# A two-layer hybrid transformer step on one core: where a finished pair of attention heads is split into its two product parts

## The chip, the cores and the metric

The kernel runs on one core of a Trainium2 chip, one launch per run. The metric is the device time of a run in microseconds (us). Before the change the median of three runs is 1104.95 us (1104.42 to 1105.27). The core has five engines that work through their own queues in order: TensorE (PE in the profile, with the loading of its weights shown apart as PEld), VectorE (DVE), ScalarE (ACT), GpSimd (POOL) and SyncE (SP), which here issues nearly all transfers.

## What is computed

Two layers on 512 tokens of width 1024 in float32. Both mix tokens, project with `w_out`, add, and run a gated feed-forward. The parts that the change touches are the two attentions (shapes and names are shortened):

```python
def memory_attention(q_mem, mem_n, w_mem_kv):          # 4 heads of 64, in both layers
    k, v = split(mem_n @ w_mem_kv)                     # 256 memory rows
    p = softmax(einsum('bshd,bmhd->bhsm', q, k) * 64 ** -0.5)
    return einsum('bhsm,bmhd->bshd', p, v)

def forgetting_attention(q, k, v, log_f):              # 12 heads of 64, layer 2 only
    c = cumsum(log_f)
    logits = einsum('bthd,bshd->bhts', q, k) * 64 ** -0.5 + c_t - c_s
    p = softmax(where(s <= t, logits, -inf))           # causal
    return einsum('bhts,bshd->bthd', p, v)

mixed = concatenate([main, memory_attention(...)], axis=-1)
h = h + rmsnorm(mixed @ w_out[layer], ln_mix_post[layer])
```

In layer 1 `main` is a gated spatial mix, in layer 2 it is the forgetting attention.

## The kernel before

**Products in parts.** A float32 product is taken as three products of a high and a low part (`mm3`, L189 to L193). So everything that enters a product is first *split* (`split`, L238): ACT copies the tile to the rounded high part, then DVE subtracts it to get the low part. Splits of weights are `whi`/`wlo` from `raw`, of turned probabilities `pT` from `tr`, of finished heads `mixedhi`/`mixedlo` from `f`. `last_parts` holds the two instructions of the last split written.

**Two heads per tile.** A head's output fills 64 of 128 rows. `join` (L414) adds the two halves of the output bank `o` (or `mo`) into one tile `f` that two heads, a pair, share. After the second head of a pair it hands back a function, the split of the finished `f` into `mixedhi` and `mixedlo`. There are two pairs in layer 1 and eight in layer 2 (two of the memory heads, six of the forgetting heads).

**The schedule of heads.** `attend` (L538) walks through the heads by a list of steps, and in one round it does the first half of head `u` and the second half of the head before it, `r`:

- `S3 S2 S1 S0` are the logits of `u` (PE, bank `lg`, two products each of 512, 384, 256 and 128 columns) with the row maximum (DVE, L443) and the exponential (ACT, L445); `N3 N2 N1 N0` scale the probabilities `p` by the reciprocal of their sum (DVE, L452 and L457, one of them on ACT, L455).
- `T0 T1 T2` turn the probabilities of `r` (PE transposes into `tr`, L464) and split the turned block into `pT`; `V0 V1 V2` are its products with the values (PE, L532, into `o`). `V2` ends with `join`.
- `F0` to `F4` are places for other work: pieces of the key, value and output projections (PE, with the splits of their weights), and the making of the next head's operands (`head_parts`, L1347: six copies of 128 KB and two of 4 KB into `qa`, `ka`, `qc`, `kc`, issued by SP).

Before the change the split of a finished pair is put into the list `late` and written at the next place for other work, which after `V2` is `F4`, the last step of the same round.

**The order in the queues.** What is written is then ordered by a scheduler: it merges the writing order into one queue per engine, by when it thinks that operands and buffers are ready. `tc.issue_after` (in `behind`, L247) adds an order edge on an engine and no wait: what is written in its block comes behind the named instruction in the same engine's queue. So a change of the writing order moves other instructions too. In the queues the heads of layer 2 are called f0 to f11 below; the round of head f*n* is the one in which its logits are written. Finished pairs are 0 to 5, and pair *n* is finished in the round of f(2*n*+2).

**Buffers.** `tr` banks 2, `mm` and `lg` banks 3 each; `raw` weights 4; `whi` and `wlo` 8 each. The output projection (`out_part`, L895, products `y`) is spread over the last rounds as pieces of three products per two-part step, and reads the memory pairs and pairs 0 and 1; the last four pairs are read after all heads (`mix_tail`, L920).

Of the kernel before, what the change touches and what calls it, by code (L numbers as in the profile page):

```python
# [16 lines left out]
T = 512  # L17
# [23 lines left out]
def hybrid(ctx: ExitStack, tc: tile.TileContext, i: dict, out: bass.AP):  # L41
# [11 lines left out]
    last_load, last_exp, last_parts = [None], [None], [None, None]  # L53
# [192 lines left out]
    @contextmanager  # L246
    def behind(some):  # L247

        with ExitStack() as s:
            for ins in some:  # L250
                s.enter_context(tc.issue_after(ins.ins))
            yield
# [285 lines left out]
    def attend(heads, before={}, between={}):  # L538


        steps = ("T0", "S3", "F0", "T1", "S2", "N3", "F1", "V0", "S1", "N2", "T2", "F2", "S0", "N1", "V1", "N0",
                 "F3", "V2", "F4")
        r, late = None, []
        for n, u in enumerate(list(heads) + [None]):
            more = list(between.get(n, ()))
            due = [len(more) * (x + 1) // 5 for x in range(5)]
            ahead = list(before.get(n, ()))
            done = 0
            for what in steps:
                x = int(what[1])  # L550
                if what[0] == "F":
                    for f in late + ahead[:1] + more[done : due[x]]:
                        f()
                    late, ahead = [], ahead[1:]
                    done = due[x]
                elif what[0] in "SN":
                    if u:
                        (u.logits if what[0] == "S" else u.norm)(x)
                elif r and x in r.blocks:
                    rest = (r.transpose if what[0] == "T" else r.values)(x)  # L560
                    if rest:
                        late.append(rest)
            assert not ahead
            r = u
        for f in late:
            f()
# [22 lines left out]
    def layer_a():  # L589
# [55 lines left out]
        with tc.tile_pool(name="sgu", bufs=1) as lp:  # L645
# [59 lines left out]
            mem_kv.append(mem_project(0, xs, wk))  # L705
            mixed = [None] * KT
            attend(mem_heads(0, q, mixed), between={n: take(fill, c) for n, c in enumerate((4, 4, 4, 4))})
            with tc.issue_after(last_exp[0].ins):
                for vt in (*vg.values(), us[0]):
# [492 lines left out]
    def layer_b(phase, fp):  # L1202
# [178 lines left out]
        for n, c in zip(range(12, 17), (2, 3, 3, 4, 4)):  # L1381
            between[n] = take(more, c)
        assert not fill and not more
        attend(heads, before, between)
        return mix_tail(1, mixed, ys)

# [113 lines left out]
```

## Time and profile before

| what | value |
|---|---|
| median of three runs | 1104.95 us (1104.42 to 1105.27) |
| the profiled execution: time, span | 1104.7 us, 1103.0 us |
| mean granted TensorE clock | 0.999 |
| busy: DVE, ACT, POOL | 888.0 us, 679.6 us, 23.9 us |
| heads of layer 1 (first logits to last join) | about 49 to 87 us |
| heads of layer 2: forgetting heads f0 to f11 | first logits at 613.2 us, last join at 722 us |
| splits of finished pairs, `mixedhi` and `mixedlo` | 10 each, median 620 and 686 ns |

The profile shows one execution on the chip. In the timeline a row is: start in us from the span's start, duration in us, engine, line, operation, tiles written and read, shape, count, and in brackets the idle time of the engine just ahead of the row and what ended it. Matmuls are pipelined: a product of 512 columns is shown with some 0.4 us but the next one starts 0.23 us later, so the time that PE loses is read from start to start. In the table of stages the columns are, for each engine, its busy time and the number of its instructions.

### The profile page before, as it was taken

The page shows a single profiled execution, that of the slowest core. Times are in us where ns is not written, and L with a number is a line of the kernel's source. Part 1 is how long each engine was busy: PE and PEld are TensorE (multiplying, and loading weights), DVE is VectorE, ACT ScalarE, POOL GpSimd, SP SyncE. Part 2 cuts the span into 40 slices and gives each one's busy share as a digit, 9 for nine tenths or more (in the row PEclk, how much of TensorE's full clock was granted, in tenths as well). Part 3 has the DMA queues.
Part 4 walks back from the last instruction along what each step waited for, and adds up shares of the span by engine and source line. Part 5 has one row for each costly group of instructions (what it writes and reads, how often), then busy time and mean ns, then how long its engine had stood idle before and what let it go on. Part 6 is the DMA issues. An engine that isn't in the chain of part 4 may idle for free.

```text
span 1103.0 us, 19497 instructions
## 1 busy us (share of the span) xinstructions
PE 1095.4 (99%) x7363; PEld 1001.7 (91%) x7363; DVE 888.0 (81%) x1750; ACT 679.6 (62%) x1428; POOL 23.9 (2%) x40
## 2 busy tenths in 40 slices
PE   9999999999999999999999999999999999999998
PEld 8998889999899899998988998889999899899996
DVE  7879759897698588797968789868997698588776
ACT  7776578664365254477747788868665266255454
POOL 0000000000000000001000000000000000000000
PEclk9999999999999999999999999999999999999999
DMA  7521331334135133245222654531235134233232
GB/s 271 160 79 58 115 115 39 116 115 138 54 115 145 54 109 115 77 153 175 71 82 61 154 136 119 148 115 40 78 97 153 58 115 132 61 113 117 77 97 77
DMA packets 64021, 118.65 MB, mean 108 GB/s; under 512 B 5236, under 2 KB 40072, under 8 KB 63928
## 3 DMA queue, kind: packets, MB, share of 16 engines
q1 hardware_dynamic: 63032, 116.57, 35.0%
q8 instruction: 58, 0.95, 0.4%
q0 software_dynamic: 192, 0.52, 0.2%
q10 hardware_dynamic: 704, 0.32, 0.1%
q14 instruction: 35, 0.29, 0.1%
HBM read 105.23 MB, written 2.10 MB: 97 GB/s over the span
## 4 chain that ended last, share of the span: by engine, by line
PE 93%; DVE 3%; ACT 2%; DMA 1%; issue 1%; SPq 0%; DVEq 0%; ACTq 0%
PE y L191 10%; PE y L192 10%; PE y L193 10%; PE a L191 5%; PE a L193 5%; PE a L192 5%; PE ps L191 4%; PE ps L193 4%; PE ps L192 4%; PE x L193 3%; PE x L191 3%; PE x L192 3%; PE e L191 3%; PE e L193 3%; PE e L192 3%; PE v L191 2%
## 5 line engine op out<-in xcount | busy, mean ns | idle before, releaser
L239 ACT CAST whi<-raw 128x512 fp32r<-128x512 f32 x460 | 277.6, 620 | 260.8 <-PE y L193 118.5
L239 DVE TENSOR_TENSOR wlo<-raw,whi 128x512 fp32r<-128x512 f32 x460 | 307.5, 689 | 116.2 <-ACT whi L239 114.0
L191 PE MATMUL y<-whi,fhi 128*128 128x512 f32 (+1 forms) x356 | 139.7, 393 | 0.0
L193 PE MATMUL y<-whi,flo 128*128 128x512 f32 (+1 forms) x356 | 139.4, 392 | 0.0
L192 PE MATMUL y<-wlo,fhi 128*128 128x512 f32 (+1 forms) x356 | 139.3, 391 | 0.0
L193 PE MATMUL x<-xshi,wlo 128*128 128x256 f32 x320 | 89.9, 281 | 0.0
L191 PE MATMUL x<-xshi,whi 128*128 128x256 f32 x320 | 89.8, 281 | 0.0
L191 PE MATMUL a<-xshi,whi 128*128 128x256 f32 x320 | 89.8, 281 | 0.0
L192 PE MATMUL x<-xslo,whi 128*128 128x256 f32 x320 | 89.8, 281 | 0.0
L192 PE MATMUL a<-xslo,whi 128*128 128x256 f32 x320 | 89.8, 281 | 0.0
L193 PE MATMUL a<-xshi,wlo 128*128 128x256 f32 x320 | 89.7, 281 | 0.0
L193 PEld LDWEIGHTS y<-whi,flo 128*128 128x128 f32 x356 | 66.9, 188 | 15.5 <-DVE flo L239 0.2
L192 PEld LDWEIGHTS y<-wlo,fhi 128*128 128x128 f32 x356 | 67.0, 188 | 14.8 <-DVE wlo L239 0.2
L191 PEld LDWEIGHTS y<-whi,fhi 128*128 128x128 f32 x356 | 66.9, 188 | 14.7
L191 PE MATMUL ps<-xshi,whi 128*128 128x256 f32 (+1 forms) x224 | 68.4, 306 | 0.0
L192 PE MATMUL ps<-xslo,whi 128*128 128x256 f32 (+1 forms) x224 | 66.7, 298 | 0.0
L193 PE MATMUL ps<-xshi,wlo 128*128 128x256 f32 (+1 forms) x224 | 66.4, 298 | 0.0
L191 PEld LDWEIGHTS a<-xshi,whi 128*128 128x128 f32 x320 | 60.3, 189 | 0.3
L192 PEld LDWEIGHTS a<-xslo,whi 128*128 128x128 f32 x320 | 60.2, 188 | 0.4
L191 PEld LDWEIGHTS x<-xshi,whi 128*128 128x128 f32 x320 | 60.3, 189 | 0.0
L193 PEld LDWEIGHTS x<-xshi,wlo 128*128 128x128 f32 x320 | 60.3, 188 | 0.0
L193 PEld LDWEIGHTS a<-xshi,wlo 128*128 128x128 f32 x320 | 60.3, 189 | 0.0
(303 smaller groups left out, 3079.3 us busy)
## 6 DMA issues: line engine op xcount, KB each, us to landing
raw<-in_w_gate SPq DMA_DIRECT2D x44, 512.0 KB, 3.5
raw<-in_w_up SPq DMA_DIRECT2D x44, 512.0 KB, 3.6
raw<-in_w_down SPq DMA_DIRECT2D x44, 512.0 KB, 4.1
raw<-in_w_out SPq DMA_DIRECT2D x16, 512.0 KB, 3.6
raw<-in_w_b_q SPq DMA_DIRECT2D x8, 512.0 KB, 4.5
raw<-in_w_a_v SPq DMA_DIRECT2D x6, 512.0 KB, 8.1
raw<-in_w_a_u SPq DMA_DIRECT2D x6, 512.0 KB
raw<-in_w_v SPq DMA_DIRECT2D x6, 512.0 KB, 3.6
```

The costliest lines, as they stand in the source:

```text
L191: PE.matmul(o, w[0], x[0], start=start, stop=False, skip_group_check=more)
L192: PE.matmul(o, w[0], x[1], start=False, stop=False, skip_group_check=more)
L193: return PE.matmul(o, w[1], x[0], start=False, stop=stop, skip_group_check=more)
L239: last_parts[:] = A.copy(hi, src), (eng or V).tensor_sub(lo, src, hi)
```

## The change

The split of a finished pair no longer stands at the next place for other work. It waits in `late` until `F1` of the next round, and is written there behind the two instructions of the split of that round's `T1` (`parted`). What is still in `late` after the last round is written then, as before.

```diff
-        r, late = None, []
+        r, late, parted = None, [], []
...
                 x = int(what[1])
                 if what[0] == "F":
-                    for f in late + ahead[:1] + more[done : due[x]]:
+                    if x == 1:
+                        with behind(parted):
+                            for f in late:
+                                f()
+                        late = []
+                    for f in ahead[:1] + more[done : due[x]]:
                         f()
-                    late, ahead = [], ahead[1:]
+                    ahead = ahead[1:]
...
                 elif r and x in r.blocks:
                     rest = (r.transpose if what[0] == "T" else r.values)(x)
+                    if what[0] == "T":
+                        parted = list(last_parts)
                     if rest:
                         late.append(rest)
```

No instruction is added or taken away on any engine. Eight of the ten splits move: pair 0 of layer 1, and in layer 2 both memory pairs and pairs 0 to 4. The last pair of each layer stays, since no round follows it. With the eight the scheduler moves others; on PE the order changes only from head f6's round on.

**First place: DVE at the start of f7's round**, where pair 2 has just been finished (`ISA` is the masking with row maximum, its second row the reading of the maximum; `vals` are the parts of the values). Before:

```order
L239 TENSOR_TENSOR vals_6904<-vf_8150,vals_6904 128x4x64
L239 TENSOR_TENSOR wlo_8415<-k_8381,whi_8414 128x512
L443 ISA p_8409,nmx_6973<-lg_8406,neg 128x512
L443 ISA nmx_6973 128x1
L239 TENSOR_TENSOR mixedlo_8278<-f_8279,mixedhi_8277 128x512
L239 TENSOR_TENSOR pT_8399<-tr_8397,pT_8398 128x512
L443 ISA p_8432,nmx_6973<-lg_8429,neg 128x384
L443 ISA nmx_6973 128x1
L239 TENSOR_TENSOR pT_8422<-tr_8420,pT_8421 128x512
L443 ISA p_8457,nmx_6973<-lg_8454,neg 128x256
```

With the change, the same stretch on DVE:

```order
L239 TENSOR_TENSOR vals_6904<-vf_8150,vals_6904 128x4x64
L443 ISA p_8407,nmx_6973<-lg_8404,neg 128x512
L443 ISA nmx_6973 128x1
L239 TENSOR_TENSOR pT_8397<-tr_8395,pT_8396 128x512
L443 ISA p_8430,nmx_6973<-lg_8427,neg 128x384
L443 ISA nmx_6973 128x1
L239 TENSOR_TENSOR wlo_8569<-raw_8566,whi_8568 128x512
L239 TENSOR_TENSOR pT_8420<-tr_8418,pT_8419 128x512
L443 ISA p_8457,nmx_6973<-lg_8454,neg 128x256
L443 ISA nmx_6973 128x1
L239 TENSOR_TENSOR mixedlo_8278<-f_8279,mixedhi_8277 128x512
```

The pair's low part went from ahead of the first turned block to behind the maximum of 256 columns, and a weight's low part (`wlo` of `raw_8566`), which stood some ten rows further down, came up between the two turned blocks.

**Second place: ACT in f9's round**, where pair 3 has been finished (`y` is the evacuation of an output projection bank). Before:

```order
L239 CAST mixedhi_8494<-f_8496 128x512
L239 CAST pT_8621<-tr_8620 128x512
L445 ACTIVATE p_8632,sm_6978<-p_8632,nmx_6977 128x512
L239 CAST pT_8644<-tr_8643 128x512
L445 ACTIVATE p_8655,sm_6978<-p_8655,nmx_6977 128x384
L445 ACTIVATE p_8681,sm_6978<-p_8681,nmx_6977 128x256
L239 CAST pT_8688<-tr_8687 128x256
L455 ACTIVATE p_8632<-p_8632,sm_6978 128x512
L914 COPY y_8716<-y_8668 128x512
L445 ACTIVATE p_8655,sm_6978<-p_8655,nmx_6977 128x128
```

With the change:

```order
L239 CAST pT_8619<-tr_8618 128x512
L445 ACTIVATE p_8630,sm_6978<-p_8630,nmx_6977 128x512
L239 CAST pT_8642<-tr_8641 128x512
L445 ACTIVATE p_8653,sm_6978<-p_8653,nmx_6977 128x384
L239 CAST mixedhi_8494<-f_8496 128x512
L239 CAST pT_8688<-tr_8687 128x256
L445 ACTIVATE p_8681,sm_6978<-p_8681,nmx_6977 128x256
L455 ACTIVATE p_8630<-p_8630,sm_6978 128x512
L445 ACTIVATE p_8653,sm_6978<-p_8653,nmx_6977 128x128
L921 COPY y_8716<-y_8668 128x512
```

The pair's high part went from the first place to behind the exponential of 384 columns, and the last exponential now stands ahead of the bank's evacuation.

**Third place: PE at the start of f10's round** (`tr` are the transposes of `T0` and `T1` of f9, `lg` the first logits of f10, `y` the output projection). Before:

```order
L191 MATMUL y_8725<-whi_8572,mixedhi_7485 128x512
L192 MATMUL y_8725<-wlo_8573,mixedhi_7485 128x512
L512 MATMUL lg_8741<-ka_8659,qa_8658 128x512
L464 MATMUL tr_8732<-ident,p_8655 128x128
L464 MATMUL tr_8732<-ident,p_8681 128x128
L464 MATMUL tr_8732<-ident,p_8655 128x128
L464 MATMUL tr_8732<-ident,p_8632 128x128
L513 MATMUL lg_8741<-kc_6945,qc_6943 128x512
```

With the change:

```order
L464 MATMUL tr_8757<-ident,p_8653 128x128
L464 MATMUL tr_8757<-ident,p_8630 128x128 x2
L191 MATMUL y_8725<-whi_8578,mixedhi_7763 128x512
L192 MATMUL y_8725<-wlo_8579,mixedhi_7763 128x512
L193 MATMUL y_8725<-whi_8578,mixedlo_7764 128x512
L191 MATMUL y_8725<-whi_8582,mixedhi_8026 128x512
L192 MATMUL y_8725<-wlo_8583,mixedhi_8026 128x512
L512 MATMUL lg_8741<-ka_8659,qa_8658 128x512
L513 MATMUL lg_8741<-kc_6945,qc_6943 128x512
```

The first logits of f10 went from ahead of the eight transposes to behind them and five more products.

On SP the queue changes as well. In f6's, f8's and f10's operands a step came ahead of the copies into `qa` and `ka`: for f6 a load of `w_out` (`raw_8782`), for f8 the copy into f9's `qc_6944`, for f10 two loads of `w_out` and the copy into f11's `qc_6944`. A `qc` tile can only be overwritten when the logits two heads earlier have read it.

## The prediction

> **What bounds the kernel.** I read the page's first part, then a table of stages over the heads of layer 2, then the timeline of PE there.
>
> ```profile
> PE 1095.4 (99%) x7363; PEld 1001.7 (91%) x7363; DVE 888.0 (81%) x1750; ACT 679.6 (62%) x1428; POOL 23.9 (2%) x40
> ```
>
> PE is busy for all but 7.6 us of the span, and the change gives it no product more or less. It can only win what PE loses by waiting near the moved splits. The stages (us from the span's start; PE, PEld, DVE, ACT, POOL busy; clock; DMA share; GB/s):
>
> ```profile
> 657.70:673.20 15.50, 15.50 (x93) 13.52 (x92) 13.17 (x40) 12.78 (x33) 0.00 (x0) 1.00 0.50 124
> 673.20:688.40 15.20, 14.80 (x83) 12.25 (x82) 15.00 (x42) 13.46 (x34) 0.00 (x0) 1.00 0.58 140
> 688.40:705.50 17.10, 16.50 (x89) 13.23 (x88) 15.31 (x47) 15.57 (x39) 0.00 (x0) 1.00 0.63 168
> 705.50:722.90 17.40, 17.40 (x94) 14.76 (x93) 10.59 (x26) 10.55 (x26) 0.00 (x0) 1.00 0.24 71
> ```
>
> Until 673 PE is never idle, whatever DVE and ACT do; after 705 again. Between, in the rounds of f7 to f10, DVE is busy for 15.00 of 15.20 us and then, with ACT, for about nine tenths, and PE has gaps. Here they are, each with the row ahead of it:
>
> ```profile
> 676.25 0.39 PE L532 MATMUL o<-pT,vals 128*128 128x512 f32 x1
> ...
> 676.83 0.50 PE L532 MATMUL o<-pT,vals 128*128 128x512 f32 x1 [0.19 <-DVE pT L239]
> ...
> 681.26 0.40 PE L193 MATMUL k<-shi,wlo 128*128 128x512 f32 x1
> ...
> 681.87 0.63 PE L464 MATMUL tr<-ident,p 128*128 128x128 f32 x4 [0.21 <-DVE p L457]
> ...
> 688.43 0.40 PE L512 MATMUL lg<-ka,qa 128*128 128x512 f32 x1
> ...
> 688.67 0.40 PE L513 MATMUL lg<-kc,qc 68*128 68x512 f32 x1
> ...
> 691.29 0.40 PE L193 MATMUL y<-whi,mixedlo 128*128 128x512 f32 x1
> ...
> 692.16 0.50 PE L532 MATMUL o<-pT,vals 128*128 128x512 f32 x1 [0.48 <-ACT pT L239]
> ...
> 697.01 0.40 PE L512 MATMUL lg<-ka,qa 128*128 128x512 f32 x1
> ...
> 697.48 0.63 PE L464 MATMUL tr<-ident,p 128*128 128x128 f32 x4
> ...
> 703.28 0.39 PE L193 MATMUL y<-whi,mixedlo 128*128 128x512 f32 x1
> ...
> 703.71 0.39 PE L532 MATMUL o<-pT,vals 128*128 128x256 f32 x1
> ```
>
> From start to start a step of 512 columns takes 0.24 us where nothing waits (688.43 to 688.67). The five steps here take 0.58, 0.61, 0.87, 0.47 and 0.43 us, so they lose 0.34, 0.37, 0.63, 0.23 and 0.19: **1.76 us together, 0.16% of the run**. A measurement of this kernel can tell about 0.2% (2.2 us) from no change, so even all of it would hardly be seen.
>
> **What the change does, place by place.** No instruction is added: 8 splits of 0.62 us on ACT and 0.69 us on DVE change places (durations below), and others move round them.
>
> *The rounds before f6.* Layer 2's memory pairs and pairs 0 and 1 move where PE's order stays and PE has no gap: 0. That cover is gone only if the turned blocks or the maxima came over a microsecond later, and they come earlier or at most one split later.
>
> *Layer 1.* One pair moves, PE's order stays. On DVE, three weight parts (one more than before) and a maximum now stand where the pair's part stood, so the first turned block comes one instruction, 0.6 us, later, and the second maximum about 1.4 us, behind both turned blocks.
>
> ```profile
> 74.45 0.68 DVE L239 TENSOR_TENSOR pT<-tr,pT 128x512 fp32r<-128x512 f32 x1
> ...
> 75.56 0.61 PE L493 MATMUL mo<-pT,memv 128*128 128x512 f32 x2
> ...
> 82.23 0.40 PE L192 MATMUL ps<-alo,whi 128*128 128x512 f32 x1
> ...
> 82.69 0.50 PE L493 MATMUL mo<-pT,memv 128*128 128x512 f32 x1
> ```
>
> The part now ends at 75.13 and would end at some 75.7; the first product, at 75.56, takes the high part and the second, 0.24 us later, the low one. So PE waits for 0 to 0.3 us. The next wait, at 82.69 (0.46 − 0.24 = 0.22 us), ends with ACT and takes up what PE lost before it. Between 0 and +0.4 us I take **+0.1**.
>
> *f7's round, pair 2.*
>
> ```profile
> 675.49 0.68 DVE L239 TENSOR_TENSOR mixedlo<-f,mixedhi 128x512 fp32r<-128x512 f32 x1
> ...
> 676.10 0.68 DVE L239 TENSOR_TENSOR pT<-tr,pT 128x512 fp32r<-128x512 f32 x1
> ...
> 677.24 0.69 DVE L239 TENSOR_TENSOR pT<-tr,pT 128x512 fp32r<-128x512 f32 x1
> ...
> 677.81 0.79 PE L532 MATMUL o<-pT,vals 128*128 128x384 f32 x4
> ...
> 681.17 0.55 DVE L457 TENSOR_SCALAR p<-p,sm 128x256 f32<-128x256 f32 x2
> ```
>
> With the pair's part out of the way the turned block starts 0.61 us earlier, at 675.49, and the 0.34 us at 676.83 go. But a weight's part takes the free place ahead of the second turned block, so that one still starts at about 677.2 and ends at 677.9, and the products at 677.81, now due at 677.47, wait some 0.2 to 0.3 us for it. And the end of the round hangs on the scaling at 681.17: all of DVE's work ahead of it is the same, with no idle time in it, so it ends when it did, and the transposes at 681.87 wait the longer for all that PE has won. **0**, between −0.34 and 0.
>
> *f9's round, pair 3.*
>
> ```profile
> 691.00 0.62 ACT L239 CAST mixedhi<-f 128x512 fp32r<-128x512 f32 x1
> ...
> 691.53 0.58 ACT L239 CAST pT<-tr 128x512 fp32r<-128x512 f32 x1
> ...
> 691.66 0.69 DVE L239 TENSOR_TENSOR mixedlo<-f,mixedhi 128x512 fp32r<-128x512 f32 x1 [0.20 <-ACT mixedhi L239]
> ...
> 695.58 0.59 ACT L914 COPY y<-y 128x512 f32<-128x512 f32 x1 [0.30 <-PE y L193]
> ...
> 696.59 0.17 DVE L452 RECIPROCAL sm<-sm 128x2 f32<-128x2 f32 x1 [0.33 <-ACT p L445]
> ```
>
> ACT reaches the turned block 0.53 us earlier (691.00 in place of 691.53), which is most of the 0.63 us at 692.16. What stays of it is decided by DVE's end: two idle times on DVE go, 0.20 us (it no longer waits for the pair's high part) and 0.33 us (the last exponential goes ahead of the evacuation at 695.58). So f9's scaling may end 0.53 us earlier, **−0.53**; between −0.63 and 0.
>
> *f10's round.*
>
> ```profile
> 697.25 0.68 DVE L424 TENSOR_TENSOR f<-o,f 64x512 f32<-64x512 f32 x1
> ...
> 697.87 0.48 PE L513 MATMUL lg<-kc,qc 68*128 68x512 f32 x1
> 698.15 1.31 ACT L239 CAST pT<-tr 128x512 fp32r<-128x512 f32 x2 [0.99 <-PE tr L464]
> ...
> 698.38 0.69 DVE L443 CUSTOM_DVE_ANT_0 p<-lg,neg 128x512 f32<-128x512 f32 x1 [0.46 <-PE lg L513]
> ...
> 703.30 0.35 ACT L239 CAST pT<-tr 128x256 fp32r<-128x256 f32 x1
> ```
>
> Before, DVE takes the first maximum at 698.38, while ACT copies the turned blocks. Now the logits stand behind eight transposes and five products: four transposes take 0.39 us (697.48 to 697.87), so 0.8 + 5 x 0.24 = 2.0 us behind the first transpose, where they began 0.47 us ahead of it. With their second product, which ended at 698.35 or so, the first maximum moves from 698.38 to some 700.2, 1.8 us. Meanwhile DVE can do the two turned blocks, 1.3 us at 0.68 us each, but only once ACT has copied the first, 1.3 us behind the first transpose, so DVE idles about 0.8 in place of 0.46 us. By the idle time that is 0.8 − 0.46 = +0.34 us, by the maximum 1.8 − 1.3 = +0.5 us; all of the softmax follows, up to the third turned block at 703.30, for which PE waits at 703.71. I take **+0.35**; between 0 (three more products stand ahead of that wait now) and +1.0.
>
> *Behind f10* DVE falls to 10.59 of 17.40 us, and nothing there waits for pair 4.
>
> Sum: 0.1 + 0 − 0.53 + 0.35 = −0.1 us on the profiled 1104.7 us. That execution lies 0.25 us below the median of 1104.95, so on the median I forecast **1104.8 us**: the gaps change places and the time stays. Its own range, by the ends above, is −1.0 to +1.4 us, 1104.0 to 1106.3.
>
> The Trainium skill, Perfetto Trace Analysis, section Identifying Performance Opportunities, says that a kernel generally gets faster by the most-contended engine getting faster. Its section Optimization Strategy says to find the gaps on the engine and make what ends them start sooner. The first speaks against this change, which takes nothing from DVE in its fullest stage (15.00 of 15.20 us), and would make the sum 0; the second speaks for it, and would make it rival A's.
>
> **The rivals.**
>
> *A: the two gaps that end behind a moved split are won for good.* 0.34 + 0.63 us, and the first product after each gap was slow as well (0.50 in place of 0.39 us of duration), which makes about −1.2 us: 1103.8 us on the median. For it: 676.83 and 692.16 name the turned block directly behind the split. Against it: DVE's full stage, from which the next wait (681.87) follows. At the most all five gaps go, and a little of the starts behind them: −2.4 us, 1102.6 us.
>
> *B: SP's queue holds the heads' operands.* For f8 the copies into `qa` and `ka` now stand behind a copy that waits until f7's logits have read `qc`, and for f10 behind that of f9 and behind two loads.
>
> ```profile
> 675.54 0.60 SPq L1356 DMA_DIRECT2D qa<-whi  x1
> ...
> 677.69 0.28 PE L513 MATMUL lg<-kc,qc 68*128 68x128 f32 x1
> ...
> raw<-in_w_out SPq DMA_DIRECT2D x8, 512.0 KB, 4.1
> ka<-whi SPq DMA_DIRECT2D x24, 128.0 KB, 2.4
> ```
>
> f8's copies began at 675.54; now they begin after 677.97 and one issue of 0.5 us, the last `ka` is issued some 1.9 us later, at 680.4, and lands 2.4 us after that at 682.8. The first logits of f8, behind eight transposes, are due at 683 to 683.5: half a microsecond of slack. For f10 it comes out at about 698.3 against 699. If a load takes the DMA engines in between and a copy lands like a load, 4.1 us after its issue, PE waits 1.2 us at f8 and 1.0 us at f10, and DVE, whose maxima are late then, does not make it good: +2.2 us on the forecast, 1107.0 us, and more if f9 and f11 are held as well; f8 alone gives 1106.0. It decides from a landing of about 3 us on, and makes the change slower.
>
> *C: the change does next to nothing*, since the scheduler fills the freed places with other work (as with the weight's part in f7's round) and two of the ten splits stay. It gives the median, 1104.95, and lies within the forecast's range.
>
> **How the numbers follow.** Forecast with C 0.70, A 0.16, B 0.14. From A about a quarter reaches beyond −2.2 us: faster 0.04. From B a third lies beyond 1107.2 us (0.05), and 0.02 are for what I have not seen: slower 0.07. Within 0.2%: 0.89. The range leaves out the outer half of A and of B: 1103.4 to 1106.6.
>
> **What would show it.** Right: the rows of `pT` at f7 and f9 start some 0.5 us earlier against their transposes; the gaps at 676.83 and 692.16 are smaller; new ones stand at the second turned block of f7, at f8's first transposes and at f10's first logits; PE's lost time over 673 to 706 stays within 1 us of 1.76; DVE still full in 673 to 688. Wrong for A: that lost time falls below 0.8 us. Wrong for B: a gap ahead of `lg<-ka,qa` ended by a DMA, or SP issuing f8's `ka` later than 681. The forecast fails if DVE has idle time in the rounds of f7 and f8 that I don't see, or if a wait grows in a round before f6.

## The result, and the profile after

The changed kernel takes **1107.06 us** (median of 11 runs, 1106.1 to 1109.48) against 1104.95 us in runs of the kernel before beside it: a ratio of 1.0021, 95% interval 1.0014 to 1.0029, that is 1.5 to 3.2 us slower. The forecast was 1104.8 us, from 1103.4 to 1106.6. The profiled execution of the changed kernel took 1108.34 us (span 1106.6), 1.3 us more than its median. That surplus has to be kept apart from the change.

The page's first part for the changed kernel, busy times by engine:

```profile
PE 1097.7 (99%) x7362; PEld 1003.7 (91%) x7363; DVE 887.7 (80%) x1750; ACT 679.5 (61%) x1428; POOL 24.3 (2%) x40
```

PE is busy for 2.3 us more than before (1095.4) while DVE and ACT have the same work. So most of the added time is no idle time of PE: PE does the same products and is shown busy for longer.

The stages of the changed kernel over the heads of layer 2, cut 2.9 us later than before, which is what its instructions are late there (us from the span's start; PE, PEld, DVE, ACT, POOL busy; clock; DMA share; GB/s):

```profile
660.60:676.10 15.50, 15.50 (x93) 13.40 (x92) 13.08 (x40) 13.06 (x34) 0.00 (x0) 1.00 0.52 130
676.10:691.30 15.20, 14.18 (x80) 11.78 (x78) 14.90 (x43) 13.22 (x33) 0.00 (x0) 1.00 0.43 98
691.30:708.40 17.10, 17.04 (x95) 14.29 (x94) 15.16 (x46) 15.33 (x39) 0.00 (x0) 1.00 0.73 190
708.40:725.80 17.40, 17.40 (x94) 14.65 (x94) 10.98 (x27) 11.19 (x27) 0.00 (x0) 1.00 0.27 87
```

In the second row, f7's and f8's rounds, PE is now idle for 15.20 − 14.18 = 1.02 us (before 0.40), in the third, f9's and f10's, for 0.06 (before 0.60). Together 1.08 against 1.00 us: at the place that the change moves, the gaps changed their places and the time stayed, as forecast. PE's waits in these rounds, from its timeline:

```profile
680.83 0.61 PE L532 MATMUL o<-pT,vals 128*128 128x384 f32 x3 [0.16 <-DVE pT L239]
685.14 1.06 PE L464 MATMUL tr<-ident,p 128*128 128x128 f32 x8 [0.62 <-DVE p L457]
686.44 0.50 PE L532 MATMUL o<-pT,vals 128*128 128x512 f32 x1 [0.24 <-ACT pT L239]
```

**Where the time came from instead.** I took the start of each PE instruction in one profile and subtracted the start of the same instruction (same names and size, same count) in a profile of the kernel before. This *shift*, as the median over a stretch, stays level where nothing is lost, and steps where something is. Against the profile of the kernel before that was taken in the first experiment, the shift of the changed kernel (its profile in the same experiment) is +1.21 us over 12 to 70 us, +1.52 over 90 to 200, +1.53 over 590 to 612, +1.96 over 613.5 to 640, +1.79 over 709 to 745 and +2.87 over 1072 to 1090. So there are five terms: +1.21 in the first 12 us, **+0.31** in layer 1's memory heads, **+0.43** in one step at f0's first logits, **−0.18** in all of the rounds from there to 709 us, and **+1.08** spread over 750 to 1070 us, where no instruction was moved.

### The profile page after: what moved, and what is told of

Its sections match the earlier page's. It is cut to its first block, busy times and chain, and to the rows that moved or that the text cites. A ratio compares the mean times of both kernels' runs of the same rounds, so it can differ in the third digit from the quotient of the medians.

```text
span 1106.6 us, 19505 instructions
## 1 busy us (share of the span) xinstructions
PE 1097.7 (99%) x7362; PEld 1003.7 (91%) x7363; DVE 887.7 (80%) x1750; ACT 679.5 (61%) x1428; POOL 24.3 (2%) x40
## 4 chain that ended last, share of the span: by engine, by line
PE 95%; DVE 2%; DMA 1%; ACT 1%; issue 1%; SPq 0%; DVEq 0%; ACTq 0%
PE y L191 10%; PE y L193 10%; PE y L192 10%; PE a L191 5%; PE a L192 5%; PE a L193 5%; PE ps L191 4%; PE ps L193 4%; PE ps L192 4%; PE x L191 3%; PE x L193 3%; PE x L192 3%; PE e L191 3%; PE e L193 3%; PE e L192 3%; PE v L191 2%
## 5 line engine op out<-in xcount | busy, mean ns | idle before, releaser
L192 PEld LDWEIGHTS x<-xslo,whi 128*128 128x128 f32 x320 | 60.2, 188 | 0.0
```

What stands on the lines that cost most here:

```text
L192: PE.matmul(o, w[0], x[1], start=False, stop=False, skip_group_check=more)
```

## The experiments

The table gathers the shifts' steps in the runs' profiles. "2063 steps" is the time from the first to the last start of the same 2064 PE instructions of layer 2's feed-forward stage, behind 780 us, in which PE never waits. Layer 1 has the same stage from 200 to 490 us: 288.1 to 288.6 us in every run but the four with a changed distance. One wait stands in it, at 237 us, which differs from execution to execution. The 35 steps round it take 4.17 to 4.62 us in those runs, all the others together 283.91 to 283.94 us in each of them. In the profile of the kernel before:

```profile
237.30 0.19 PEld L191 LDWEIGHTS e<-t,whi 128*128 128x128 f32 x1 [0.26 <-ACT s L1073]
```

| run | median us | ratio to before, interval | layer 1 heads | f0's logits | rounds to 709 | 2063 steps |
|---|---|---|---|---|---|---|
| before again | 1104.85 | 0.9996 (0.9987–1.0004) | 0 | 0 | 0 | 286.57 |
| changed again | 1107.36 | 1.0020 (1.0011–1.0029) | +0.31 | +0.43 | −0.18 | 287.55 |
| layer 1 alone | 1105.25 | 1.0000 (0.9991–1.0008) | +0.30 | 0 | −0.03 | 286.57 |
| layer 2 alone | 1106.02 | 1.0006 (0.9997–1.0015) | +0.01 | +0.58 | −0.33 | 287.55 |
| memory pairs alone | 1105.58 | 1.0007 (0.9998–1.0016) | +0.01 | +0.28 | +0.22 | 286.56 |
| heads' pairs alone | 1105.65 | 1.0007 (0.9997–1.0016) | +0.01 | 0 | +0.07 | 287.55 |
| before, low parts first | 1104.80 | 1.0001 (0.9992–1.0010) | +0.01 | 0 | +0.05 | 286.55 |
| changed, low parts first | 1106.57 | 1.0016 (1.0007–1.0025) | +0.32 | +0.54 | −0.04 | 287.55 |
| changed, 64 bytes | 1105.37 | 1.0006 (0.9997–1.0015) | +0.25 | +0.42 | −0.28 | 287.60 |
| before, 64 bytes | 1105.26 | 1.0003 (0.9994–1.0012) | 0 | −0.03 | +0.03 | 287.92 |
| before, 96 bytes | 1105.00 | 1.0002 (0.9993–1.0011) | −0.02 | −0.10 | +0.26 | 287.38 |
| before, 224 bytes | 1105.37 | 1.0006 (0.9997–1.0015) | +0.04 | 0 | +0.03 | 287.69 |
| changed, load put back | 1106.42 | 1.0012 (1.0003–1.0021) | +0.31 | 0 | +0.07 | 287.60 |

### 1. Which part of the change costs

Both kernels unchanged, and the change in one layer alone. For the halves, `attend` got a flag:

```diff
-    def attend(heads, before={}, between={}):
+    def attend(heads, before={}, between={}, moved=True):
...
-                    if x == 1:
+                    if x == 1 and moved:
                         with behind(parted):
                             for f in late:
                                 f()
                         late = []
+                    if not moved:
+                        for f in late:
+                            f()
+                        late = []
```

The kernel before:

> The kernel of before, unchanged, as the yardstick for one more set of runs. It should give 1105.0 us, within 0.5, and ratio 1.000. Its profile says what of the +1.9 us that the first profile of the change shows ahead of 12 us (first products late, clock 0.50 over 9 to 12 us) is a matter of the single execution: if starts differ from execution to execution, the first logits of f0 here need not stand at 613.2 us, but may stand up to 2 us later.

The changed kernel:

> The changed kernel, unchanged, beside the kernel of before on one chip. Theory 'place' (the moved splits cost time where they stand) and theory 'all along' (something of the whole program, such as its start or where its buffers lie) both expect 1107 us and ratio 1.002; theory 'chance' (the two sets of runs differed by their executions) expects 1105.0 to 1105.6 and ratio under 1.0005. The profile tells the first two apart: 'place' wants the shift against before to grow by over 1.5 us between the logits of the first memory head (49 us) and 87 us, or between the first logits of f0 and 709 us; 'all along' wants it at 10 us or spread over the span.

`moved=False` in layer 2's call:

> The change in layer 1's four memory heads alone; layer 2 as before. Theory 'place, layer 1': 1107 us, shift of 1.5 to 2 us between 49 and 95 us. Theory 'place, layer 2': 1105.0 within 0.4. My prediction gave this part +0.1 (0 to +0.4): 1105.0 to 1105.4.

`moved=False` in layer 1's call:

> The change in layer 2's heads alone; layer 1 as before. Theory 'place, layer 2': 1107 us, with 1.5 to 2 us more lost by TensorE in 640 to 709 us than before's 1.76. Theory 'place, layer 1' and my prediction: 1104.7 within 0.5. If both halves give 1106, the cost is of both places; if both give 1105, it is of neither and sits in how the whole comes out.

The difference is real: the changed kernel came out at 1107.36 us in this set. "Chance" falls as its cause. Layer 1 alone costs +0.30 us, in one stretch; layer 2 alone +1.07 us in the median. Neither ratio is clear of noise (both intervals take in 1), and together they give 1.4 of the 2.4 us. "All along" got one half right: the shift grows in a part of the program that the change doesn't touch.

Layer 1's part, on PE in the profile of layer 1 alone:

```profile
75.44 0.73 PE L493 MATMUL mo<-pT,memv 128*128 128x512 f32 x2
75.66 0.19 PEld L493 LDWEIGHTS mo<-pT,memv 128*128 128x128 f32 x1 [0.26 <-DVE pT L239]
...
82.87 0.50 PE L493 MATMUL mo<-pT,memv 128*128 128x512 f32 x1 [0.24 <-ACT pT L239]
```

The two products now take 0.73 in place of 0.61 us, because the second waits for its low part, and from the first of them to the product of the next turned block 7.43 us pass in place of 7.13 (82.69 − 75.56). The second wait did not take the first one up, as I had allowed for: it grew too, from 0.22 to 0.40 us from start to start. ACT's copy, which ends it, starts 0.30 us later against the first product (82.25 − 75.44 in place of 82.07 − 75.56).

What the start costs differs from execution to execution of one program. The shift over 12 to 70 us was 0 and 0.36 us in the two profiles of the kernel before and 1.21 and 2.25 us in the two of the changed kernel. In the fourteen profiles beside the yardstick it lies between 0.06 and 2.37 us. Here is the worse kind, windows of the changed kernel's first profile:

```profile
5.00:9.00 4.00, 2.78 (x14) 1.74 (x13) 2.46 (x5) 2.54 (x5) 0.00 (x0) 0.95 0.98 350
9.00:12.00 3.00, 3.00 (x16) 3.00 (x16) 2.70 (x6) 2.30 (x4) 0.00 (x0) 0.50 1.03 406
```

The third number from the end is the granted clock: 0.50 for three microseconds, in which PE starts 16 products. The kernel before had 26 there, at 1.00:

```profile
9.00:12.00 3.00, 3.00 (x26) 2.96 (x26) 2.60 (x5) 2.28 (x5) 0.00 (x0) 1.00 1.03 408
```

### 2. Which pairs, and whether it is where the weight parts lie

In layer 2 the memory pairs and the heads' pairs were moved separately. The tile pool hands out 8 buffers for high weight parts and 8 for low ones, to whichever is free first. With the heads' pairs moved, that order comes out otherwise from the rounds of layer 2 on: of the program's last 2343 products, 802 take their stationary part (the one that stays in PE while the other streams through) from another buffer than before, by the addresses in the built programs. With the memory pairs or layer 1 moved, none does. That gave a new theory, "places": PE's pace depends on where the stationary operand lies. To try it without moving any instruction, the low parts' buffers were put ahead of the high ones.

```diff
-                    if x == 1:
+                    stay = len(heads) == 4 or n >= 6
+                    if x == 1 and not stay:
...
+                    if stay:
+                        for f in late:
+                            f()
+                        late = []
```

Memory pairs alone (`n >= 6`):

> Only the two memory pairs of layer 2 are split late; the heads' pairs and layer 1 as before. In program order the load of a key weight (raw from in_w_k) then stands on SP ahead of the copies of f0's and f1's operands, as in the changed kernel, and no weight part lies elsewhere than before. Theory 'queue': the first logits of f0 come 0.4 to 0.6 us later against before than the products just ahead of them, their row says that they waited for ka; nothing is lost behind 709 us; 1105.4 us in all. Theory 'heads' (the moved pairs of the heads cost): no shift anywhere, 1104.95.

Heads' pairs alone (`n < 6`):

> Only the heads' pairs 0 to 4 of layer 2 are split late; the memory pairs and layer 1 as before. SP's rows ahead of f0 are those of before; the weight parts behind 700 us lie in the places that they have in the changed kernel. Theory 'queue': no wait at f0. Theory 'places' (a product's pace depends on where its weight part lies): 0.2 to 0.3 us won between f0's first logits and 709 us, and 1.0 to 1.1 us lost, evenly, between 750 and 1070 us: +0.8, 1105.75 us. Rival 'softmax order' (something of the heads' rounds): the loss stands between 640 and 709 us.

The other order of the buffers, two lines ahead of layer 1's first weights:

```diff
+        wp.tile([P, 1024], F32, tag="raw", name="raw_first", bufs=4)
+        wp.tile([P, 536], F32R, tag="lo", name="lo_first", bufs=8)
+        wp.tile([P, 536], F32R, tag="hi", name="hi_first", bufs=8)
```

In the kernel before:

> The kernel of before with one thing changed: the buffers of the low weight parts lie ahead of those of the high parts in SBUF, in place of behind them. Every engine's order is that of before, row for row. Theory 'places': the pace of the 256-column products of a, x and e behind 750 us changes from 117.5 ns by several tenths of a nanosecond, up or down, and the run by 0.5 to 2 us, spread evenly; no gap moves. Rival (the pace is set by what runs beside the products, that is by the order): 117.5 ns within 0.1, and 1104.95 us.

In the changed kernel:

> The changed kernel with the low weight parts' buffers ahead of the high ones'; order unchanged against the changed kernel. Theory 'places': behind 750 us the pace is not 118.2 ns, and its distance from the run before (low parts first, too) is not the +0.7 ns that the two kernels had; it may have either sign. The loss of 0.3 in layer 1 and of 0.4 to 0.6 at f0 stay. Rival: +0.7 ns and +1.05 us between the two remain, whatever the places.

The first two told the parts apart as "queue" and "places" had it, with sizes that were off. The memory pairs bring a step at f0 (+0.28 in place of 0.4 to 0.6, and another +0.22 by 709 us) and no change of pace; the heads' pairs bring no step at f0 and 1.03 us behind 750. But the heads' pairs win nothing in the rounds (+0.07 in place of −0.2 to −0.3). The gain of 0.2 to 0.3 that the first experiment shows there stands only in runs that have lost time at f0, and I read it as that loss being made up. That isn't shown: with the memory pairs alone, the loss at f0 is not made up but grows.

The windows of the feed-forward stage of layer 2, from the same instruction to the same, count for count. The kernel before:

```profile
783.91:1070.48 286.57, 286.57 (x2064) 269.68 (x2063) 229.49 (x391) 148.78 (x293) 0.00 (x0) 1.00 0.34 105
```

The changed kernel:

```profile
786.63:1074.17 287.54, 287.54 (x2064) 270.56 (x2063) 229.39 (x391) 148.65 (x293) 0.00 (x0) 1.00 0.34 105
```

Memory pairs alone:

```profile
784.79:1071.34 286.55, 286.55 (x2064) 269.59 (x2063) 229.34 (x391) 148.67 (x293) 0.00 (x0) 1.00 0.34 105
```

Heads' pairs alone:

```profile
783.61:1071.15 287.54, 287.54 (x2064) 270.55 (x2063) 229.48 (x391) 148.74 (x293) 0.00 (x0) 1.00 0.34 105
```

PE is busy all the time, the clock is 1.00, the DMA load, DVE and ACT are nearly the same, and the same 2064 instructions take 0.97 us longer, to a hundredth the same in every kernel of these two experiments with the changed buffers. It is no scatter: from the stage's first start, each of the 2064 starts in the two profiles of the kernel before agrees to 1 ns, and so it does in the two of the changed kernel and in the heads' pairs alone.

Step by step, between the two kernels' profiles of experiment 1, a step being the time from the product ahead to a product's own start: some 956 steps of the 256-column products whose own and whose next stationary part lie where they lay before differ by −0.06 us in sum; some 723 whose own or next stationary part lies elsewhere by +0.96 us; and the 385 steps of `y`, whose stationary parts are no weights, by +0.07. If the product ahead is counted as well, 898 steps have a stationary part elsewhere, and they differ by +0.98 us, the other 781 by −0.08. If the step is taken to the next start in place of from the one before, the first split is 0.71 against 0.19 us, so the division between neighbours is less sure than the sum.

But the other order of the buffers changed nothing: 286.55 and 287.55 us. Taken as it was written, "places" had failed, and the order was left as a cause. The swap, though, had changed the distance between a high and a low part from +17,152 to −17,152 bytes (eight buffers of 2,144 bytes), and both are multiples of 256 bytes. So a finer theory was left, "remainder": the pace depends on the distance modulo 256 bytes. Its rival, "slots", has it that the sequence of the buffers counts and not where they lie.

### 3. Another distance between the buffers, with the order kept

```diff
+        wp.tile([P, 1024], F32, tag="raw", name="raw_first", bufs=4)
+        wp.tile([P, 536], F32R, tag="hi", name="hi_first", bufs=8)
+        wp.tile([P, 16], F32, tag="pad", name="pad", bufs=1)
```

The third line leaves 64 bytes free between the groups (24 and 56 elements for 96 and 224 bytes). Every engine's order stays what it was in the kernel that it is put into, row for row.

> The changed kernel with 64 bytes left free between the high and the low weight parts' buffers, which so stand at another distance modulo 256 bytes; every engine's order is that of the changed kernel. Swapping the two groups (a distance that is a multiple of 256 bytes) had left the pace as it was, 117.5 ns for the order before and 118.2 for the order of the change. Theory 'remainder' (the pace of a high and a low weight part read in turn depends on the remainder of their distance by 256 bytes; in the runs so far 117.4 ns at a remainder of 32, 118.7 at 64, 115.8 at 128): behind 750 us 116.5 to 117.3 ns in place of 118.2, about 2 us won there, and 1 to 3 us in the stretch of layer 1 from 100 to 600 us; 1103 to 1105 us. Theory 'slots' (it is the sequence of buffers itself, not where they lie): 118.2 ns and 1107 us.

> The kernel of before with the same 64 bytes between the two groups. Theory 'remainder': layer 1 as in the run above (1 to 3 us won, since both kernels have the same places there), but behind 750 us 117.7 to 118.0 ns in place of 117.5, so that the changed kernel is there the faster of the two; 1102.5 to 1104 us in all. Theory 'slots': 117.5 ns, 1104.95 us.

> The kernel of before with 96 bytes between the groups. Theory 'remainder', by the same table: 117.9 ns in layer 1 in place of 118.4 (some 0.8 us won) and 116.7 ns behind 750 us in place of 117.5 (1.0 to 1.5 us won): 1102.5 to 1103.5 us. Theory 'slots': no change.

> The kernel of before with 224 bytes between the groups (which is 32 less, modulo 256). Theory 'remainder': 116.5 to 117.5 ns in layer 1 (2 us or more won) and 118.0 ns behind 750 us (0.7 us lost): 1103 to 1104.5 us. Theory 'slots': no change.

The kernel before with 64 bytes, layer 1's stage and layer 2's:

```profile
202.07:489.23 287.16, 287.16 (x2064) 270.30 (x2063) 233.26 (x400) 151.51 (x302) 0.00 (x0) 1.00 0.34 104
783.19:1071.11 287.92, 287.92 (x2064) 270.98 (x2063) 229.58 (x391) 148.81 (x293) 0.00 (x0) 1.00 0.34 105
```

The same two windows of the kernel before, the first of them new here:

```profile
201.59:489.95 288.36, 288.31 (x2064) 271.14 (x2063) 233.44 (x400) 151.35 (x302) 0.00 (x0) 1.00 0.34 104
783.91:1070.48 286.57, 286.57 (x2064) 269.68 (x2063) 229.49 (x391) 148.78 (x293) 0.00 (x0) 1.00 0.34 105
```

Layer 1's windows differ by 1.2 us, but some 0.3 of it is the wait at 237 us. Without the 35 steps round it the stage takes 283.04 us with the 64 bytes, in both kernels, in place of 283.91 to 283.94: 64 bytes win 0.9 us there. 96 and 224 bytes win 0.7 and 0.5 us (283.19 and 283.44). In layer 2 the 64 bytes lose 1.35 us, with no instruction moved. They also shift what lies behind the low parts, such as the moving operand of some `e` products; but 1.1 of the 1.35 us stand in the products of `a` and `x`, of whose operands and banks only the low weight part lies elsewhere. That **shows** that the place of the weight parts alone is worth more than the 0.97 us in question, and "slots" falls. And with these 64 bytes the changed kernel is no longer slower behind 780 us but 0.3 us faster than the kernel before (287.60 against 287.92). The medians, 1105.37 and 1105.26 us, lie 0.1 us apart in place of 2.5; the stage behind 780 us accounts for 1.3 us of that, the rest was not traced.

The rule that I had read out of the runs, by the remainder modulo 256, failed in layer 2: it wanted 64 bytes to be worth +0.2 to +0.5 ns a product there and 96 bytes to be worth −0.8, and every distance tried in it came out slower there, by 0.8 to 1.35 us over the stage. In the changed kernel, where it wanted some 2 us less, the 64 bytes left the stage as it was (287.60 against 287.55). Layer 2 of the kernel before, at 286.57 us, has simply the quickest of the places that were tried; its own layer 1 needs 288.2 to 288.4 for as many steps. What it is about a place that makes a product quicker stays open.

### 4. The load on SP

In the changed kernel SP issues the load of a key weight ahead of the copies of f0's and f1's operands. SP's queue in the changed kernel:

```profile
606.44 0.47 SPq L1366 DMA_DIRECT2D kc<-cc  x1
608.99 0.34 SPq L152 DMA_DIRECT2D raw<-in_w_k  x1
609.42 0.52 SPq L1363 DMA_DIRECT2D qa<-whi  x1
609.99 0.59 SPq L1363 DMA_DIRECT2D qa<-wlo  x1
610.67 1.19 SPq L1363 DMA_DIRECT2D ka<-whi  x2
```

Ahead of the load SP stands for 2 us, until DVE has made the weight's low part (`wlo`) that frees a `raw` buffer, and everything behind it stands too. In the kernel before, the load went behind all eight copies:

```profile
606.45 1.19 SPq L1356 DMA_DIRECT2D ka<-whi  x2
...
610.30 0.54 SPq L152 DMA_DIRECT2D raw<-in_w_k  x1
```

So f0's `ka` is issued at 610.67 in place of 606.45. The whole profile is 2.4 us late there; what the load costs `ka` is the other 1.8 us. f0's logits wait for it, PE in the changed kernel:

```profile
616.07 0.47 PE L512 MATMUL lg<-ka,qa 128*128 128x512 f32 x1 [0.23 <-DMA ka<-whi]
```

To tell the load from the later split of the memory pairs, only the load was put back, by an order edge:

```diff
             def load():
-                w.extend(prepared(i["w_k"][m], (KT, P)))
+                with behind(copied if m == 4 else []):
+                    raw = loaded(i["w_k"][m])
+                w.extend(weight_parts(raw, (KT, P)))
```

(`copied` holds the copies of f0's and f1's operands. On ACT the split of a query part, `whi` from `q`, moves by one row with it.)

> The changed kernel with one row of SP put back: the load of the key weight (raw from in_w_k) stands behind the copies of f0's and f1's operands again; on PE, DVE and POOL every row is that of the changed kernel. Theory 'queue': the wait of f0's first logits for ka goes, so that the shift against before does not grow between 612 and 614 us (it grew by 0.43 to 0.58); the loss in layer 1 (0.3) and the slower pace behind 750 us (1.0) stay: 1106.6 to 1106.9 us. Rival (the wait comes from the later end of the memory pairs' split itself): the 0.4 to 0.6 us at f0 stay, 1107.1 to 1107.4 us.

The step at f0 is gone (0.00 us) with the split left where the change has it. PE in this kernel:

```profile
615.46 0.48 PE L512 MATMUL lg<-ka,qa 128*128 128x512 f32 x1
```

The logits start without a wait. "Queue" is shown. The median, 1106.42, lies 0.2 us below the expected span; it is 1.7 us above the 1104.72 of the kernel before beside it, where 1.65 to 1.95 over 1104.95 were expected. The rounds behind f0 give +0.07 us now in place of −0.18, as with the heads' pairs alone. In the changed kernel, then, over half of the loss at f0 goes again in these rounds.

## Why the prediction was wrong, step by step

- **What bounds the kernel: right.** PE without a gap outside f7 to f10, DVE full in f7 and f8. It led to the wrong search, though: a kernel whose PE is 99% busy can also lose by PE's own pace, and the prediction had no term for that.
- **Layer 1, +0.1 (0 to +0.4): within its bounds, one step wrong.** It is +0.25 to +0.32 us in six profiles. The wait for the low part came as said; that the next wait "takes up what PE lost before it" failed, since ACT's copy came later too.
- **The rounds before f6, 0: this step failed.** "Layer 2's memory pairs and pairs 0 and 1 move where PE's order stays and PE has no gap" looked at PE, DVE and ACT and not at SP, although one load changes its row there; the changes of SP's queue that are listed with the change lack this row, too. It costs 0.42 to 0.58 us at f0 in the changed order (0.28 with the memory pairs alone). The condition that was named for the cover to go, turned blocks or maxima over a microsecond late, was the wrong one: it was an operand's transfer. A wait that grows in a round before f6 is the sign of failure that the prediction itself named.
- **f7's round, 0 (−0.34 to 0): right for the turned blocks, wrong for the round's end.** The turned block does go into the pair's part's place and the second one starts when it did. In the changed kernel, then in the kernel before:

```profile
678.41 0.68 DVE L239 TENSOR_TENSOR pT<-tr,pT 128x512 fp32r<-128x512 f32 x1
...
679.49 0.69 DVE L239 TENSOR_TENSOR wlo<-raw,whi 128x512 fp32r<-128x512 f32 x1
680.09 0.68 DVE L239 TENSOR_TENSOR pT<-tr,pT 128x512 fp32r<-128x512 f32 x1
...
682.57 1.29 DVE L239 TENSOR_TENSOR wlo<-raw,whi 128x512 fp32r<-128x512 f32 x2
...
683.86 0.67 DVE L239 TENSOR_TENSOR wlo<-raw,whi 128x512 fp32r<-128x512 f32 x1
684.45 0.54 DVE L457 TENSOR_SCALAR p<-p,sm 128x256 f32<-128x256 f32 x2
```

```profile
679.31 1.28 DVE L239 TENSOR_TENSOR wlo<-raw,whi 128x512 fp32r<-128x512 f32 x2
...
680.59 0.68 DVE L239 TENSOR_TENSOR wlo<-raw,whi 128x512 fp32r<-128x512 f32 x1
681.17 0.55 DVE L457 TENSOR_SCALAR p<-p,sm 128x256 f32<-128x256 f32 x2
```

  Less the shift of 2.9 us that this profile has there, the two rows of `pT` stand at 675.5 and 677.2, to a tenth where the prediction put them. But the scaling stands at 681.55 in place of 681.17. "All of DVE's work ahead of it is the same" failed: four low parts of weights stand there in place of three, the one between the turned blocks being added to the three and not taken from them. So the transposes wait 0.62 us, and f8 has a wait of 0.24 that was not foreseen. In idle time the two rounds lose 0.62 us more.
- **f9 −0.53 and f10 +0.35: the first right, the second wrong.** ACT reaches f9's turned block at 693.85, that is 690.95 less the shift, where 691.00 was forecast, and the gap of 0.48 us is gone. f10's new wait does not come. Together the two rounds win 0.54 us of idle time in place of 0.18. The errors of f7/f8 and of f9/f10 cancel; with the heads' pairs alone the whole stretch is worth +0.07 us.
- **Behind f10, 0: this step failed, and it is the largest term.** No wait for pair 4 shows there, as said, and yet +1.0 us comes from there, because the moved splits change the order in which weight buffers come free, and 802 of the last 2343 products take their stationary part from elsewhere.
- **Rival B (SP's queue holds operands): the mechanism was right, at another place.** It was priced for f8 and f10, where no logits wait for a DMA; it happened at f0. **Rival A** did not happen: nothing was won for good.

In sum, by the shifts of the changed kernel's second profile: 0.31 + 0.43 − 0.18 + 1.08 = +1.64 us, of which the prediction had −0.1. The two sets measured +2.1 and +2.4, with intervals of 1.5 to 3.2 and 1.2 to 3.2, which take the sum in. The rest, half a microsecond or somewhat more, was not found in a place of its own and need not be real: with the low parts first the same sum gives 1.9 us and the median 1.7, with the load put back 1.5 and 1.7. The start is the only other stretch that differs. Whether it is later on average in the changed kernel is open: the seven profiles with the memory pairs moved have shifts of 0.15 to 2.37 us there, the seven others (beside the yardstick) 0.06 to 0.84, and the program up to there is the same.

No version here is faster than the kernel before by what a measurement can tell. What could be put together, layer 1's 0.9 us with 64 bytes and layer 2's places as they were, would need the buffers to lie otherwise in the two layers, and would bring 0.1%; that was not tried.

## What to carry to other kernels

When a scheduler and pools decide the order, compare the rows of *every* engine from the first difference on, the DMA-issuing ones first: a load that waits for a buffer holds all transfers issued behind it. And when one execution unit is busy 99% of the time, a change of a few splits can cost more by giving out the buffers in another order than by anything at its own place, so a difference of 0.1 to 0.2% need not mean that the idea was bad: compare the start of the same instruction in both traces, look where the difference grows, and give the buffers other places once before judging.

## What the runs showed of the hardware that was not expected

- The pace of PE's float32 products depends on where the stationary operands lie: the same 2063 steps took 286.55 to 287.92 us in layer 2 (138.9 to 139.6 ns a step), and the stage of layer 1 without the steps round its one wait 283.04 to 283.94, at a clock of 1.00. For one set of places it repeats: in layer 2 each start agrees to 1 ns between two profiles of one kernel, and the stage to 0.05 us between kernels. Where the moving operand or the output bank alone changed, no difference of more than 0.13 us in sum showed.
- Of some 10,500 groups of three products (high part twice, then low) in eight profiles, about 200 took 340 or 341 ns in place of some 355. In most of these the low part lay 128 bytes from the high one, modulo 256, but only about one in eight of the 1,500 groups with that remainder is so quick. It may be a part of the answer and isn't the whole.
- In two of the fifteen profiles the granted clock fell to 0.50 from 9 to 12 us, after PE had waited three or four times by up to 0.66 us ahead of its first products; in the other thirteen it was 1.00 there. What brings the drop on is open: with layer 2 alone PE waited as often and for longer (twice some 0.7 us), and the clock stayed at 1.00. These two had the largest shifts at the start, 2.25 and 2.37 us, against 1.21 us at the most elsewhere. The changed kernel's own profile is one of them, which fits its surplus over its median. Of the 114 runs of the kernel before beside the experiments, the 13 with a mean clock of 0.998 or less took 1106.02 to 1106.97 us, the other 101 at most 1105.96, with a median of 1104.8. The change's own loss isn't this: in experiment 1 the runs at 0.999 or 1.000 alone have medians of 1107.1 (8 runs) and 1104.7 (26).
